# A recurrent scan's VectorE steps, joined over two heads and traced later

## Chip, cores and metric

The kernel runs on one core of a Trainium2 chip. The metric is device time in microseconds (us) of one execution. The engines are TensorE (PE in the profile: matmuls; its weight loads are PEld), VectorE (DVE), ScalarE (ACT), GpSimd (POOL) and SyncE (SP, which only issues DMAs). Each engine runs its own list of instructions in the order in which the list was written, and waits at an instruction until what it needs is there.

## The reference

One decoder layer on a sequence of 1024 tokens of width 1024, in float32. It normalises x, projects it into eight groups of 1024 channels, mixes over time in two ways, gates and adds the two results, projects back and adds to x. A squared-ReLU MLP of width 4096 and a last norm follow.

```python
xa, ga, q, f, v, g, m_a, m_b = split(h @ w_in)
xa = causal_depthwise_conv(xa)
# RG-LRU: a linear recurrence over time, channel by channel
r = sigmoid(blocks(xa, w_r) + b_r);  i = sigmoid(blocks(xa, w_i) + b_i)
log_a = -8 * r * softplus(-lam);     a = exp(log_a)
u = sqrt(max(-expm1(2 * log_a), 0)) * (i * xa)
h_t = a_t * h_(t-1) + u_t
y_a = h * gelu(ga)
# HGRN2: gated linear attention with 8 heads, decay f per key channel
o = rms_norm(hgrn2(silu(q), k(f), log f(f), v))
y_b = o * silu(g)
x = x + (sigmoid(m_a) * y_a + sigmoid(m_b) * y_b) @ w_out
```

## The kernel before

**Passes and pairs.** Time is cut into two passes `c` of 512 tokens (`NC`). In each pass a loop over `p` (L695) handles four pairs: 256 channels, that is two "heads" `s` of 128 channels (one per partition) by 512 tokens. After the four pairs comes the output projection of the pass (`out_proj`), and after both passes the MLP.

**Products.** Every float32 product is made from three matmuls of rounded parts, `mm3` (L123 to L125): high by high, high by low, low by high. The weights are loaded raw and cut into a high part by ACT (L78, names `wH`) and a low part by DVE (L79, names `wL`), three weight tiles ahead; a new raw tile is loaded when an old one has been cut.

**One pair, in PE's order.** PE's instructions within a pair are pinned to the order in which they are traced (`pin`, L117): the `q` projection, two steps of `f`, the RG-LRU's gate products `pr` and `pi` for both heads (L350 to L356), the rest of `f`; then the generator `gates` yields the projections `g`, `mb`, `ga`, `ma` in steps of six matmuls, and `hgrn` places its own small matmuls between them: `GO` says how many steps go ahead of each. The small ones are the first batch of scores (`blocks`, L415, three sets), the second batch (L533 and L544), the transposes `pk` (L570), the state products `pkv` (L579) and the outputs `po` (L603 and L606). L544 multiplies `kk` and `qf`, which DVE writes at L525 and L526 and ACT at L523 and L524. L606 reads the states `sn`, which DVE writes at L587 and L589.

**What orders the other engines.** The framework writes each engine's list at build, by a planner with estimated durations: whenever an engine is free it takes, of the instructions whose inputs are there, the one that was traced first. `high_priority(n)` counts an instruction as traced n earlier. The weight cuts have 400, and the RG-LRU has 300 (L707), ahead of everything else of its pair. The lists are fixed at run time.

**The RG-LRU** (`rg_lru`, L347 to L376). For each head: ACT computes the sigmoid of `pr` and its tanh into `w` (L358, L359) and the sigmoid of `pi` into `ig` (L361). DVE takes the maximum with 0 (L363), adds 1 (L365), takes the reciprocal (L366); ACT takes the square root of `w` (L367); DVE multiplies by the convolved input (L368), forms 2 w rec (L369), multiplies (L370), forms 2 rec - 1 (L371) and runs the scan along time (L373). POOL carries the last value into the next pass (L375). `w`, `ig` and `rec` are 128x512 tiles with one buffer each (tags `rw`, `ri`, `rr`), so head 1 follows head 0. Only L655 in `gates` reads the result `h`.

**The score chain** (`f_of`, L389, and `hgrn`, L402 to L558). DVE forms the decays `f` (L397, L399), then a long chain of products (all through the helper at L405) that scales queries and keys for the score levels; after the first batch of scores it copies those into `dd` (L426, L434), and writes `kk` and `qf` (L525, L526), `t64` and `t128` (L552, L558). POOL copies `dd` into the score matrix `scT` (L510), which L603 reads.

**Buffers.** A tile in a tag with one buffer has to wait until the last reader of the tile before it in that tag is done. The tags `rw` and `ri` also hold the states `sn` (L582), `rr` also holds a transposed key tile (L573), `on` holds the attention output (L561) and `g1` a gate (L635).

Of the kernel before, what the change touches and what calls it, by code (L numbers as in the profile page):

```python
# [13 lines left out]
AF = mybir.ActivationFunctionType  # L14
ALU = mybir.AluOpType
# [3 lines left out]
P = 128  # L19
D = 1024  # L20
S = 1024
T = 512
# [16 lines left out]
PV_LB, PV_CB, PV_BR, PV_BI, PV_LAM, PV_CW, PV_HG = 0, 8, 16, 24, 32, 40, 72  # L39
# [4 lines left out]
def trunk(ctx: ExitStack, tc: tile.TileContext, x, wts, mlp, pv, gains, mask_f, mask_u, out):  # L44
    nc = tc.nc
    V, A, G, PE = nc.vector, nc.scalar, nc.gpsimd, nc.tensor
# [13 lines left out]
    def bank(tag, name):  # L60
        return ps.tile([P, 512], F32, tag=tag, name=name, bufs={"pj": 4, "sc": 2, "hg": 2}[tag])
# [49 lines left out]
    def next_w():  # L111
        used[0] += 1
        return get_w(used[0] - 1)
# [3 lines left out]
    def pin(ins):  # L117
        if pinned[0]:
            tc.keep_in_program_order(ins)

    def mm3(o, ah, al, bh, bl, first, last, goes_on=False):
        how = {"skip_group_check": True} if goes_on else {}
        pin(PE.matmul(o, ah, bh, start=first, stop=False, **how))  # L123
        pin(PE.matmul(o, ah, bl, start=False, stop=False, **how))  # L124
        pin(PE.matmul(o, al, bh, start=False, stop=last, **how))  # L125
# [4 lines left out]
    pvt = const.tile([P, PV_N], F32, tag="pvt", name="pvt")  # L130
# [26 lines left out]
    def a2_set(pool, name):  # L157
        return [
            [pool.tile([P, 4, T], F32R, tag="a2", name=f"{name}{q}{h}", bufs=4) for h in range(2)] for q in ("H", "L")
        ]  # L160
# [17 lines left out]
    def mt(tag, name, shape=(P, T), dt=F32, bufs=1):  # L178
        return m.tile(list(shape), dt, tag=tag, name=name, bufs=bufs)
# [4 lines left out]
    def small_inputs():  # L184
        nc.sync.dma_start(pvt, pv)
        nc.sync.dma_start(mf, mask_f)
        mu32 = mt("kT", "mu32", (P, 4, P)).rearrange("p a b -> p (a b)")[:, : 7 * 32]
        mu32 = mu32.rearrange("p (i b t) -> p i b t", i=7, b=1)
        nc.sync.dma_start(mu32, mask_u)
        return mu32  # L190
# [5 lines left out]
    lb, omlb, sp4 = par[:, 0, :], par[:, 1, :], par[:, 2, :]  # L196
# [35 lines left out]
    hcar = const.tile([P, 8], F32, tag="hcar", name="hcar")  # L232
# [10 lines left out]
    def first_norm(c):  # L243
        dst = a2_set(a2h, f"hT{c}")
        xts = []
        for tt in range(4):
            r = c * 4 + tt
            xt = mt(X_TAGS[tt], f"x{r}", (P, D)) if c == 0 else tile_x(f"x{r}")
            nc.sync.dma_start(xt, x[r * P : (r + 1) * P, :])
            xts.append(xt)  # L250
            if c == 0 and tt == 0:
                gain0.append(gain_tile(0))
            if c == 0 and tt < 3:
                raws.append(load_w(seq[tt]))
        xns = {}

        def rows(tt):
            xns[tt] = mt("f" if tt % 2 == 0 else "tmp", f"xn{c}{tt}", (P, D))
            norm_rows(xts[tt], xns[tt], gain0[0], f"x{c}{tt}")

        def weights(n):
            if c == 0:
                fill_w(n)

        rows(0)
        weights(1)
        transposed(xns[0], dst, 0, f"x{c}0")
        rows(1)
        weights(2)
        for tt in range(1, 4):  # L270
            if tt < 3:
                rows(tt + 1)
            transposed(xns[tt], dst, tt, f"x{c}{tt}")
        weights(3)
        in_order[0] = False
        hT.append(dst)
# [14 lines left out]
    def run(steps, n=None):  # L291
        while n is None or n > 0:
            try:
                next(steps)
            except StopIteration as end:
                return end.value
            if n is not None:
                n -= 1

    def project(c, name):  # L300
        return run(project_steps(c, name))
# [44 lines left out]

    def rg_lru(c, p, xc, xh, xl):  # L347
        wh, wl = next_w()
        hs = mt("h", f"h{c}{p}", (P, 2, T))
        for s in range(2):  # L350
            u = 2 * p + s
            pr, pi = bank("pj", f"pr{c}{u}"), bank("pj", f"pi{c}{u}")
            for o, k0 in ((pr, 0), (pi, 2)):
                for k in range(2):
                    cols = slice((k0 + k) * 256 + s * P, (k0 + k) * 256 + (s + 1) * P)
                    mm3(o, wh[:, cols], wl[:, cols], xh[:, k, :], xl[:, k, :], k == 0, k == 1)  # L356
            w = mt("rw", f"rw{c}{u}")
            A.activation(w, pr, AF.Sigmoid, bias=pvt[:, PV_BR + u : PV_BR + u + 1])  # L358
            A.activation(w, w, AF.Tanh, scale=sp4[:, u : u + 1])  # L359
            ig = mt("ri", f"ri{c}{u}")  # L360
            A.activation(ig, pi, AF.Sigmoid, bias=pvt[:, PV_BI + u : PV_BI + u + 1])  # L361

            V.tensor_scalar(w, w, 0.0, None, op0=ALU.max)  # L363
            rec = mt("rr", f"rr{c}{u}")
            V.tensor_scalar(rec, w, 1.0, None, op0=ALU.add)  # L365
            V.reciprocal(rec, rec)  # L366
            A.activation(w, w, AF.Sqrt)  # L367
            V.tensor_tensor(out=ig, in0=ig, in1=xc[:, s, :], op=ALU.mult)  # L368
            V.scalar_tensor_tensor(w, w, 2.0, rec, op0=ALU.mult, op1=ALU.mult)  # L369
            V.tensor_tensor(out=ig, in0=ig, in1=w, op=ALU.mult)  # L370
            V.tensor_scalar(rec, rec, 2.0, -1.0, op0=ALU.mult, op1=ALU.add)  # L371
            h = hs[:, s, :]
            V.tensor_tensor_scan(h, rec, ig, hcar[:, u : u + 1], op0=ALU.mult, op1=ALU.add)  # L373
            if c + 1 < NC:
                G.tensor_copy(hcar[:, u : u + 1], h[:, T - 1 : T])  # L375
        return hs  # L376
# [22 lines left out]
        V.tensor_scalar(ff, ff, F_MIN, 1.0, op0=ALU.max, op1=ALU.min)  # L399
        return ff, kk  # L400

    def hgrn(c, p, q1, f, kk, v, go):  # L402

        nm = f"{c}{p}"
        mul = lambda o, a, b: V.tensor_tensor(out=o, in0=a, in1=b, op=ALU.mult)  # L405
# [67 lines left out]
        g0, g1 = 256 // c0, 256 // c1  # L473
# [35 lines left out]
        for b in range(4):  # L509
# [5 lines left out]
                op0=ALU.mult,  # L515
                op1=ALU.add,
# [41 lines left out]
        mul(t128, t64[:, 0::2], t64[:, 1::2])  # L558


        on = mt("on", f"on{nm}", (P, 8, P))  # L561
        ssq = mt("hssq", f"hssq{nm}", (P, 16), bufs=2)[:, 0:8]
        nkv = 3 if c + 1 == NC else 4
# [13 lines left out]
        for s, _ in both:  # L577
            for n in range(nkv):
                pin(PE.matmul(pkv[s][:, n * P : (n + 1) * P], kT[s][:, n, :], vn(s, n), start=True, stop=True))  # L579
        states = []  # L580
        for s, u in both:
            sn = mt(("rw", "ri")[s], f"sn{c}{u}", (P, 4, P))  # L582
            states.append([scar[:, u, :]] + [sn[:, n, :] for n in range(4)])
            for n in range(nkv):
                kv = pkv[s][:, n * P : (n + 1) * P]
                if c == 0 and n == 0:
                    V.tensor_copy(states[s][1], kv)  # L587
                else:
                    V.scalar_tensor_tensor(  # L589
                        states[s][n + 1],  # L590
                        states[s][n],
                        t128[:, 4 * s + n : 4 * s + n + 1],
                        kv,
                        op0=ALU.mult,
                        op1=ALU.add,
                    )
# [91 lines left out]
    for c in range(NC):  # L688
        if c == 0:
            first_norm(0)  # L690
            mu32 = small_inputs()
        else:
            out_proj(0, ys, res0, done0, lambda: first_norm(1))
        ys = a2_set(a2y, f"y{c}")
        for p in range(NPAIR):  # L695
            v = project_v(c, f"{c}{p}")
            px = project(c, f"xa{c}{p}")
            if c == 0 and p == 0:
                parameters()
                tc.keep_in_program_order(V.tensor_copy(mu, mu32.to_broadcast([P, 7, 8, 32])))  # L700
            xc3 = conv(c, p, px)
            pinned[0] = True
            q1 = q_of(c, p, project(c, f"q{c}{p}"))
            steps = project_steps(c, f"f{c}{p}")
            run(steps, 2)
            got = {}
            with tc.high_priority(300):  # L707
                got["h"] = rg_lru(c, p, *xc3)
            f, kk = f_of(c, p, run(steps))
            rest = gates(c, p, got, ys)  # L710
            got["on"] = hgrn(c, p, q1, f, kk, v, lambda n: run(rest, n))
            run(rest)
            pinned[0] = False
    mix.__exit__(None, None, None)
# [208 lines left out]
    for q in range(QUADS):  # L923
        n = q + 1 if q + 1 < QUADS else QUADS + QUADS - 2
# [79 lines left out]
    for kb in range(n_kb):  # L1004
        last = kb + 1 == n_kb
        qs = order[2 * kb : 2 * kb + 2]
        for half in range(2):
# [8 lines left out]
            for step, (bk, wo, uo), prs in [  # L1016
# [11 lines left out]
                for pr in prs:  # L1028
                    _, ci, cj, op = ADDS[step]
# [89 lines left out]
```

## Time and profile before

| | |
|---|---|
| median of 3 runs | 1598.83 us |
| lowest, highest | 1598.44, 1599.68 us |
| the profiled execution | 1599.54 us |
| its span | 1597.7 us |
| busy: PE, DVE, ACT, POOL | 1562.3, 1207.3, 771.7, 65.1 us |
| mean granted clock of PE | 0.995 |

The profile is one execution. Its rows give the start from the beginning of the span, the duration, the engine, the line of the kernel, the operation, the tiles written and read, and in square brackets the time that the engine idled before the instruction with what released it. Tile names are shown without their numbers, so one name stands for the tiles of all pairs. A group row gives a count and the shortest, median and longest duration in ns. The first pass runs from the start to about 490 us, the second to about 910, the MLP after that. A pair takes 104.8 us.

### The profile page before, as it was taken

Reading aid. Unit: us, or ns where it says so; the run is one execution under the profiler, and the core shown is the slowest. Engines: PE = TensorE matmul, PEld = TensorE weight load, DVE = VectorE, ACT = ScalarE, POOL = GpSimd, SP = SyncE. Lnnn points to the kernel's source line nnn. Section 1 sums busy time; section 2 is a strip of 40 time slices with the busy share of each in tenths; the row PEclk is TensorE's granted clock in tenths of the full one; section 3 lists DMA queues with packets and bytes.
Section 4 is the critical chain, followed back from the end, with each engine's and each line's share of the span. In section 5 each row is a group of like instructions: output and inputs, shape, how many; then the busy total and the mean of one; then the engine's idle time right before and its main releaser. Section 6 shows DMA issues by size and latency. Waiting matters only on the chain.

```text
span 1597.7 us, 23216 instructions
## 1 busy us (share of the span) xinstructions
PE 1562.3 (98%) x9240; PEld 1307.4 (82%) x9240; DVE 1207.3 (76%) x1751; ACT 771.7 (48%) x1210; POOL 65.1 (4%) x107
## 2 busy tenths in 40 slices
PE   7999999999999999999999998999999999999998
PEld 6888888888888888888888876888888878888886
DVE  5985966858764875947859787988888888888877
ACT  4643545446443544546435566767767732221113
POOL 0010010100100010100100100000000000000000
PEclk9999999999999999999999998999999999999999
DMA  6222213222254322322222462666666675666652
GB/s 239 95 67 94 95 64 105 81 87 87 84 166 133 97 76 82 104 76 97 67 95 92 141 206 89 266 256 242 237 250 257 224 270 229 256 248 256 257 203 106
DMA packets 57996, 246.51 MB, mean 154 GB/s; under 512 B 6688, under 2 KB 6816, under 8 KB 47136
## 3 DMA queue, kind: packets, MB, share of 16 engines
q1 hardware_dynamic: 56304, 239.27, 41.6%
q10 hardware_dynamic: 1584, 5.77, 1.0%
q8 instruction: 72, 1.18, 0.3%
q14 instruction: 36, 0.29, 0.1%
HBM read 185.24 MB, written 59.77 MB: 153 GB/s over the span
## 4 chain that ended last, share of the span: by engine, by line
PE 80%; DVE 14%; DMA 2%; ACT 2%; issue 2%; POOL 0%; DVEq 0%; POOLq 0%; SPq 0%; ACTq 0%
PE dX L123 3%; PE dX L124 3%; PE dX L125 3%; PE uX L123 3%; PE uX L124 3%; PE uX L125 3%; PE pj_ma L125 2%; PE pj_ma L123 2%; PE pj_xa L123 2%; PE pj_xa L124 2%; PE pj_ma L124 2%; PE pj_xa L125 2%; PE pv L125 2%; PE pv L124 2%; PE pj_f L125 2%; PE pj_q L125 2%
## 5 line engine op out<-in xcount | busy, mean ns | idle before, releaser
L79 DVE TENSOR_TENSOR wL<-raw,wH 128x1024 fp32r<-128x1024 f32 x160 | 194.9, 1218 | 134.6 <-ACT wH L78 133.0
L78 ACT CAST wH<-raw 128x1024 fp32r<-128x1024 f32 x160 | 167.6, 1048 | 124.3 <-PE po L124 31.7
L1031 DVE TENSOR_TENSOR acc<-acc,dX 128x512 f32<-128x512 f32 x128 | 85.0, 683 | 29.4 <-PE dX L125 28.8
L78 ACT CAST wA<-q 128x512 fp32r<-128x512 f32 x32 | 19.8, 621 | 135.0 <-PE dX L125 101.4
L1031 DVE TENSOR_TENSOR acc<-acc,dY 128x512 f32<-128x512 f32 x64 | 43.5, 685 | 15.7 <-PE dY L125 14.5
L366 DVE RECIPROCAL rr<-rr 128x512 f32<-128x512 f32 x16 | 53.5, 3345 | 0.0
L891 ACT ACTIVATE b<-b 128x512 f32<-128x512 f32 x48 | 30.2, 630 | 37.1 <-DVE b L890 37.1
L123 PE MATMUL pv<-wH,hT0H 128*128 128x256 f32 x128 | 37.2, 291 | 0.0
L124 PE MATMUL pv<-wL,hT0H 128*128 128x256 f32 x128 | 36.9, 288 | 0.0
L125 PE MATMUL pv<-wH,hT0L 128*128 128x256 f32 x128 | 36.8, 288 | 0.0
L123 PE MATMUL pv<-wH,hT1H 128*128 128x256 f32 x128 | 36.5, 285 | 0.0
L125 PE MATMUL pv<-wH,hT1L 128*128 128x256 f32 x128 | 36.2, 283 | 0.0
L124 PE MATMUL pv<-wL,hT1H 128*128 128x256 f32 x128 | 36.2, 283 | 0.0
L332 DVE SCALAR_TENSOR_TENSOR xc<-xp,pvt,xc 128x512 f32<-128x512 f32 x48 | 33.1, 745 | 0.0
L892 ACT ACTIVATE b<-b 128x512 f32<-128x512 f32 x48 | 30.0, 630 | 1.1
L79 DVE TENSOR_TENSOR wA<-q,wA 128x512 fp32r<-128x512 f32 x32 | 22.0, 688 | 10.7 <-ACT wA L78 10.1
L510 POOL TENSOR_SCALAR scT<-dd 32x256 f32<-32x256 f32 x32 | 25.4, 793 | 71.4 <-DVE dd L434 63.0
L123 PE MATMUL pj_ga<-hT0H,wH 128*128 128x512 f32 x64 | 27.1, 423 | 0.0
L523 ACT COPY kk<-kc 128x512 f32<-128x512 f32 x8 | 5.0, 623 | 45.3 <-DVE kc L405 45.3
L123 PE MATMUL pj_ga<-hT1H,wH 128*128 128x512 f32 x64 | 26.6, 416 | 0.0
L314 ACT COPY v<-pv 128x256 f32<-128x256 f32 x32 | 11.9, 370 | 29.5 <-PE pv L125 29.5
L632 ACT ACTIVATE smb<-pj_mb 128x512 f32<-128x512 f32 x16 | 9.6, 599 | 34.1 <-PE pj_mb L125 34.1
(1861 smaller groups left out, 5254.2 us busy)
## 6 DMA issues: line engine op xcount, KB each, us to landing
raw<-wts_in SPq DMA_DIRECT2D x160, 512.0 KB, 3.5
q<-mlp_in SPq DMA_DIRECT2D x64, 512.0 KB, 4.0
x<-x_in SPq DMA_DIRECT2D x8, 512.0 KB, 6.0
acc<-x ACTq DMA_DIRECT2D x8, 512.0 KB, 5.2
y_out<-acc SPq DMA_DIRECT2D x16, 256.0 KB, 2.0
xs<-x_in SPq DMA_DIRECT2D x8, 256.0 KB, 3.2
x<-xs SPq DMA_DIRECT2D x8, 256.0 KB, 2.5
x2s<-x_in SPq DMA_DIRECT2D x4, 512.0 KB, 5.2
```

The costliest lines, as they stand in the source:

```text
L78: keep(A.copy(h, src))
L79: keep(V.tensor_tensor(out=lo, in0=src, in1=h.bitcast(F32), op=ALU.subtract))
L123: pin(PE.matmul(o, ah, bh, start=first, stop=False, **how))
L124: pin(PE.matmul(o, ah, bl, start=False, stop=False, **how))
L125: pin(PE.matmul(o, al, bh, start=False, stop=last, **how))
L314: A.copy(v[:, tt, :], pp[:, :256])
L332: V.scalar_tensor_tensor(xc[:, s, :], xp[:, j : j + T], pvt[:, PV_CW + 8 * j + u : PV_CW + 8 * j + u + 1], xc[:, s, :], op0=ALU.mult, op1= ...
L366: V.reciprocal(rec, rec)
L510: G.tensor_scalar(scT[32 * b : 32 * b + 32, :, 32 * b : 32 * b + 32], dd[32 * b : 32 * b + 32, :, :], 1.0, 0.0, op0=ALU.mult, op1=ALU.add,)
L891: A.activation(b[:, at, :], b[:, at, :], AF.Relu, scale=-1.0 if at == 2 else 1.0)
L892: A.activation(b[:, at, :], b[:, at, :], AF.Square)
L1031: V.tensor_tensor(out=dst, in0=dst, in1=banks[bk, pr], op=op)
```

## The change

`rg_lru` keeps PE's products and ACT's three gate activations, now into tiles that hold both heads (`w` in tag `rw`, `ig` in tag `on`), and returns them. A new function `rg_scan` has DVE's part and one square root over both heads; the reciprocal and the scan stay one per head. `rec` lies in the tag `g1`, `h` is allocated there too. `hgrn` calls `rg_scan` after `t128` (L558), outside the high priority. The states of both heads share one tile in tag `rw`; the tag `ri` is gone.

```diff
     def rg_lru(c, p, xc, xh, xl):
         wh, wl = next_w()
-        hs = mt("h", f"h{c}{p}", (P, 2, T))
+        w = mt("rw", f"rw{c}{p}", (P, 2, T))
+        ig = mt("on", f"ri{c}{p}", (P, 2, T))
         for s in range(2):
...
-            w = mt("rw", f"rw{c}{u}")
-            A.activation(w, pr, AF.Sigmoid, bias=pvt[:, PV_BR + u : PV_BR + u + 1])
-            A.activation(w, w, AF.Tanh, scale=sp4[:, u : u + 1])
-            ig = mt("ri", f"ri{c}{u}")
-            A.activation(ig, pi, AF.Sigmoid, bias=pvt[:, PV_BI + u : PV_BI + u + 1])
-
-            V.tensor_scalar(w, w, 0.0, None, op0=ALU.max)
-            rec = mt("rr", f"rr{c}{u}")
-            V.tensor_scalar(rec, w, 1.0, None, op0=ALU.add)
-            V.reciprocal(rec, rec)
-            A.activation(w, w, AF.Sqrt)
-            V.tensor_tensor(out=ig, in0=ig, in1=xc[:, s, :], op=ALU.mult)
-            V.scalar_tensor_tensor(w, w, 2.0, rec, op0=ALU.mult, op1=ALU.mult)
-            V.tensor_tensor(out=ig, in0=ig, in1=w, op=ALU.mult)
-            V.tensor_scalar(rec, rec, 2.0, -1.0, op0=ALU.mult, op1=ALU.add)
+            A.activation(w[:, s, :], pr, AF.Sigmoid, bias=pvt[:, PV_BR + u : PV_BR + u + 1])
+            A.activation(ig[:, s, :], pi, AF.Sigmoid, bias=pvt[:, PV_BI + u : PV_BI + u + 1])
+            A.activation(w[:, s, :], w[:, s, :], AF.Tanh, scale=sp4[:, u : u + 1])
+        return w, ig, xc
+
+    def rg_scan(c, p, w, ig, xc):
+        V.tensor_scalar(w, w, 0.0, None, op0=ALU.max)
+        rec = mt("g1", f"rr{c}{p}", (P, 2, T))
+        V.tensor_scalar(rec, w, 1.0, None, op0=ALU.add)
+        A.activation(w, w, AF.Sqrt)
+        for s in range(2):
+            V.reciprocal(rec[:, s, :], rec[:, s, :])
+        V.tensor_tensor(out=ig, in0=ig, in1=xc, op=ALU.mult)
+        V.scalar_tensor_tensor(w, w, 2.0, rec, op0=ALU.mult, op1=ALU.mult)
+        V.tensor_tensor(out=ig, in0=ig, in1=w, op=ALU.mult)
+        V.tensor_scalar(rec, rec, 2.0, -1.0, op0=ALU.mult, op1=ALU.add)
+        hs = mt("h", f"h{c}{p}", (P, 2, T))
+        for s in range(2):
+            u = 2 * p + s
             h = hs[:, s, :]
-            V.tensor_tensor_scan(h, rec, ig, hcar[:, u : u + 1], op0=ALU.mult, op1=ALU.add)
+            V.tensor_tensor_scan(h, rec[:, s, :], ig[:, s, :], hcar[:, u : u + 1], op0=ALU.mult, op1=ALU.add)
...
-    def hgrn(c, p, q1, f, kk, v, go):
+    def hgrn(c, p, q1, f, kk, v, go, scan):
...
         mul(t128, t64[:, 0::2], t64[:, 1::2])
+        scan()
...
+        sn2 = mt("rw", f"sn{c}{p}", (P, 2, 4, P))
         for s, u in both:
-            sn = mt(("rw", "ri")[s], f"sn{c}{u}", (P, 4, P))
+            sn = sn2[:, s]
...
             with tc.high_priority(300):
-                got["h"] = rg_lru(c, p, *xc3)
+                rg = rg_lru(c, p, *xc3)
             f, kk = f_of(c, p, run(steps))
             rest = gates(c, p, got, ys)
-            got["on"] = hgrn(c, p, q1, f, kk, v, lambda n: run(rest, n))
+            def scan():
+                got["h"] = rg_scan(c, p, *rg)
+            got["on"] = hgrn(c, p, q1, f, kk, v, lambda n: run(rest, n), scan)
```

## Prediction

> **What bounds the kernel now.** I read the page's busy shares first.
>
> ```profile
> PE 1562.3 (98%) x9240; PEld 1307.4 (82%) x9240; DVE 1207.3 (76%) x1751; ACT 771.7 (48%) x1210; POOL 65.1 (4%) x107
> ```
>
> PE has work 98% of the span; VectorE (DVE) is idle a quarter of it. A DVE edit is worth only the time that PE waits for DVE. So next the stages that the change touches, one window for a pair of pass 0, one for the last pair of pass 0, one for a pair of pass 1 (columns: length, then busy time and instructions of PE, PEld, DVE, ACT, POOL, then PE's granted clock):
>
> ```profile
> 70.00:175.00 105.00, 104.53 (x758) 89.44 (x757) 75.09 (x114) 51.10 (x86) 7.74 (x13) 1.00 0.26 86
> 385.00:440.00 55.00, 53.12 (x478) 44.73 (x477) 44.07 (x77) 26.40 (x53) 6.39 (x11) 0.97 0.27 86
> 650.00:755.00 105.00, 105.00 (x757) 89.42 (x756) 74.91 (x113) 50.88 (x86) 5.87 (x7) 1.00 0.27 86
> ```
>
> The reader sees how little there is: PE idles 0.47 us in a pair of pass 0, 1.88 us in its last pair, nothing in pass 1. The list of PE's waits in pass 0 says for what:
>
> ```profile
> PE sc L544 <- DVE dd L434: 1.5, 3, 0.5
> PE sc L544 <- ACT wH L78: 1.0, 1, 1.0
> PE sc L533 <- DVE qb L405: 0.9, 1, 0.9
> ```
>
> All are at the second batch of scores. Then the timeline there, PE and DVE of the second pair (start, duration, idle before):
>
> ```profile
> 203.63 0.70 PE L533 MATMUL sc<-qb,kc 128*32 128x32 f32 x32
> 204.82 1.12 PE L544 MATMUL sc<-qf,kk 128*64 128x64 f32 x16 [0.49 <-DVE dd L434]
> ```
>
> ```profile
> 162.04 0.43 DVE L363 TENSOR_SCALAR rw<-rw 128x512 f32<-128x512 f32 x1 [2.90 <-ACT rw L359]
> ...
> 172.61 0.69 DVE L368 TENSOR_TENSOR ri<-ri,xc 128x512 f32<-128x512 f32 x1 [0.76 <-ACT ri L361]
> 173.60 1.22 DVE L79 TENSOR_TENSOR wL<-raw,wH 128x1024 fp32r<-128x1024 f32 x1 [0.29 <-ACT wH L78]
> ...
> 176.26 3.34 DVE L366 RECIPROCAL rr<-rr 128x512 f32<-128x512 f32 x1
> ...
> 184.19 0.67 DVE L399 TENSOR_SCALAR f<-f 128x1024 f32<-128x1024 f32 x1
> ...
> 200.12 0.21 DVE L405 TENSOR_TENSOR seg<-seg 128x16 f32<-128x16 f32 x1
> ...
> 203.99 0.68 DVE L405 TENSOR_TENSOR qf<-qb,seg 128x512 f32<-128x512 f32 x1
> ...
> 206.67 0.88 DVE L405 TENSOR_TENSOR qf<-qf,seg 128x512 f32<-128x512 f32 x1
> ```
>
> L544 multiplies qf (L526); qf ends at 203.99 + 0.68 = 204.67 and L544 starts 0.15 later. (The wait is put down to dd, but L544 does not read dd.) PE could have gone on at 203.63 + 0.70 = 204.33. From 162.04 to 204.67 DVE is one unbroken queue but for 0.76 + 0.29 us: RG-LRU first, then the score chain from L399. **The end of that queue sets PE's stall**, 0.49 us. In pass 1 the same place is just in time:
>
> ```profile
> 673.68 0.68 DVE L405 TENSOR_TENSOR qf<-qb,seg 128x512 f32<-128x512 f32 x1
> 673.91 0.70 PE L533 MATMUL sc<-qb,kc 128*32 128x32 f32 x32
> 674.54 0.33 PE L544 MATMUL sc<-qf,kk 128*64 128x64 f32 x2
> ```
>
> qf ends at 674.36; with the 0.15 us of above that is 0.03 us of slack. Nothing can be gained in pass 1, and any delay shows.
>
> **The change part by part.** *Fewer, longer DVE instructions.* The rows of the RG-LRU operations (median in ns), and two that are 1024 wide:
>
> ```profile
> L365 DVE TENSOR_SCALAR rr<-rw x16: 416/424/428, 57.6 to 854.5; 128x512 f32<-128x512 f32 x16
> L366 DVE RECIPROCAL rr<-rr x16: 3343/3344/3347, 58.6 to 855.2; 128x512 f32<-128x512 f32 x16
> L369 DVE SCALAR_TENSOR_TENSOR rw<-rw,rr x16: 676/677/679, 62.9 to 859.5; 128x512 f32<-128x512 f32 x16
> L370 DVE TENSOR_TENSOR ri<-ri,rw x16: 680/683/686, 64.6 to 860.6; 128x512 f32<-128x512 f32 x16
> L373 DVE TENSOR_TENSOR_SCAN h<-rr,hcar,ri x16: 1275/1280/1286, 65.7 to 861.9; 128x512 f32<-128x512 f32 x16
> L405 DVE TENSOR_TENSOR on<-on,hrs x8: 1225/1225/1227, 117.7 to 900.8; 128x1024 f32<-128x1024 f32 x8
> L655 DVE SCALAR_TENSOR_TENSOR g<-g,h x8: 1224/1224/1225, 114.7 to 897.7; 128x1024 f32<-128x1024 f32 x8
> ```
>
> Removed per head: three scalar forms (L363, L365, L371) at 0.42, the reciprocal 3.34, two products 0.68, L369 0.68, the scan 1.28 = 7.92; two heads 15.84 us in 16 instructions. Added per pair: three scalar forms 1024 wide at 0.67 (L399's row is that form), two reciprocals 6.68, two products at 1.225, one of L655's form at 1.22, two scans 2.56 = 14.92 us in 10. That saves 0.92 us. Independent neighbours overlap by some 0.08 us (173.60 + 1.22 = 174.82, and the next starts at 174.74), and six instructions fewer lose six overlaps: 0.44 at the other end. I take 0.7.
>
> *A later start.* The first DVE step now needs both heads. ACT and PE rows:
>
> ```profile
> 161.28 0.73 ACT L359 ACTIVATE rw<-rw,par 128x512 f32<-128x512 f32 x1
> ...
> 162.63 1.28 ACT L367 ACT_TABLE_LOAD   x1
> ...
> 170.24 0.69 ACT L358 ACTIVATE rw<-pr,pvt 128x512 f32<-128x512 f32 x1 [0.81 <-DVE ri L370]
> ```
>
> ```profile
> 162.79 0.39 PE L125 MATMUL pr<-xcH,wL 128*128 128x512 f32 x1
> ```
>
> Head 1's L358 can start when its last product ends, 162.79 + 0.39 = 163.18 (before, it waited 0.81 us for head 0's tile); with 0.69 for L358 and 0.73 for L359 the tanh of head 1 ends at 164.6, with the hand-overs 164.7. Head 0's ended at 162.01 and DVE began at 162.04. The whole block therefore starts 2.66 us later. Against that the two idle gaps go, since head 1 has its own tiles: 1.05 us.
>
> *The order on DVE.* The order is made at build: at each moment the ready instruction that was traced earliest, moved up by any priority. Tracing the block later does not push it behind the score chain; it only loses the moments in which something traced earlier is ready. Where a chain step isn't ready, a later one goes in: L552 (t64) runs at 200.12, ahead of L525 and L526 that were traced before it. The block is ready at 164.7, some ten microseconds before f. So the reciprocals still run ahead of the chain; the rest goes into its gaps and into the moment in which the chain waits for the first scores. All of it then lies ahead of qf again, and qf's end moves by +2.66 - 1.05 - 0.7 = +0.91; by the bounds of the saving 0.69 to 1.17. If the last scan alone slips behind qf (1.28 - 0.08) it is -0.3. Between those I stay near the first, since both scans are ready before the first scores are, and take 0.75.
>
> *Sum.* Pass 0, first three pairs: 3 x 0.75 = 2.2. Pass 1, four pairs: 4 x (0.75 - 0.03) = 2.9. The last pair of pass 0 has its own trouble, the next pass's norm inside its score chain:
>
> ```profile
> 410.39 1.28 DVE L147 SCALAR_TENSOR_TENSOR xn<-x,rstd_x,gain 128x1024 f32<-128x1024 f32 x1 [0.38 <-POOL rstd_x L146]
> ...
> 415.90 1.55 PE L544 MATMUL sc<-qf,kk 128*64 128x64 f32 x16 [0.97 <-ACT wH L78]
> ```
>
> It may move out (a gain: 0.49 as elsewhere, 1.5 for L147's time and wait less an overlap, and 1.5 of half clock, below: 3.5) or stay (a loss of 0.75). I take 0. Sum +5.1 us.
>
> *Costed at nothing.* One square root instead of two removes two of four 1.28 us table loads a pair: ACT is 48% busy and releases nothing that PE waits for here. The new slots: the states of L582 wait until w is done, ig sits in "on" (next written after the scores are applied, 214.60 below), rec in "g1" (next written at L639). If the block is done by qf's end, all have over 6 us. hcar's copies share POOL with the score copies:
>
> ```profile
> L510 POOL TENSOR_SCALAR scT<-dd 32x256 f32<-32x256 f32 x32 | 25.4, 793 | 71.4 <-DVE dd L434 63.0
> ```
>
> Four of these, 3.2 us from about 204.8 (after the last score copy), against some 214.2 when scT is read, just ahead of L606's 214.60 below: 6 us of cover. No DMA moves. The weight splits (L79) keep their priority, so SP's loads are freed as before, at worst one reciprocal (3.3 us) later, as now.
>
> [...] After the last pair's waits the clock halves:
>
> ```profile
> 417.00:418.00 1.00, 1.00 (x7) 0.50 0.00 0
> ```
>
> ```profile
> 207.36 1.03 PE L570 MATMUL pk<-ident,kk 128*128 128x128 f32 x8
> ```
>
> ```profile
> 419.97 1.03 PE L570 MATMUL pk<-ident,kk 128*128 128x128 f32 x8
> ```
>
> From L544 to L570 it takes 4.07 us there and 2.54 in the second pair: 1.5 us for waits of 0.92 and 0.97. [...]
>
> **Rivals.**
> 1. *The last steps slip behind qf* (the other side: faster). If both scans are placed after L526, qf ends 0.75 - 2 x 1.20 = -1.65 us, that is 1.65 earlier: the three stalls of 0.49 go (-1.5), the last pair gains 1.6 to 3.5, pass 1 nothing. -3.1 to -5.0; on the scale of the median 1594 to 1596. It wins from 0.75 us slipped per pair. For it: low priority; against it: t64's row, a gap is filled by whatever is ready.
> 2. *Nothing moves where it counts*: later start and savings cancel, within 2 us of now, 1599.
> 3. *Stalls long enough for half clock*: +1.5 us in each of seven pairs on top of 5.1: +15.6, 1614. Against it: 0.49 us stalls leave the clock at 1.00.
> 4. *The block really runs behind the chain.* Then it starts at 206.67 + 0.88 = 207.55; w is free after 11.1 us (0.67 x 2, 6.68, 1.22 x 3, less overlaps), and states must follow:
>
> ```profile
> 211.88 1.36 DVE L589 SCALAR_TENSOR_TENSOR sn<-sn,seg,pkv 128x128 f32<-128x128 f32 x4
> ```
>
> ```profile
> 214.60 0.28 PE L606 MATMUL po<-sn,qf 128*128 128x128 f32 x1
> ```
>
> The row is head 1's three states, the head before it takes about as long: 2.7 us from 218.65 is 221.4, where L606 stood at 214.60. That is 7 us a pair, 10 if the scans (3.2 us with L371's form) go ahead of the states too: +55 to +80, half clock beside it, 1655 to 1690.
>
> **How the numbers follow.** The profiled execution took 1599.54 us, span 1597.70, 0.71 above the median 1598.83 of the three runs; on the median's scale 1598.83 + 5.1 = 1603.9. Chances: forecast (+1.5 to +9) 0.50, rival 1 0.28, rival 2 0.09, rival 3 0.07, rival 4 0.06. The bound of a measurable difference is 0.2%, 3.2 us. Faster by more: 0.20 (most of rival 1). Within: 0.24 (the rest of rival 1, rival 2, the low end of the forecast). Slower: 0.56. Range: from rival 1's far end, 1594, to 1612, where the forecast's upper bound 8 x 1.17 meets half clock in a pair or two; rivals 3 and 4 are mostly left out.
>
> **What would show it.** DVE's max starts near 164.7 in the second pair, not 162.0. Reciprocals before L399. Position of the scans against L526: before it, qf ends near 205.4 and PE waits about 1.2 us at L544 in pass 0 and 0.7 in pass 1; after it, no wait. Wrong if L147 leaves the last pair's chain (3 us back), if the clock falls in other pairs, or if L606 waits for states.

## The result, and the profile after

| | before | after |
|---|---|---|
| median, lowest, highest of 6 runs, us | 1598.63, 1596.32, 1600.22 | 1606.84, 1604.79, 1608.64 |
| the profiled execution, its span, us | 1599.54, 1597.7 | 1608.64, 1606.8 |

The ratio is 1.0051, with a 95% interval of 1.0038 to 1.0064: the change costs 8.2 us. The two profiled executions are 9.1 us apart, a little more than the medians. In the changed kernel the lines behind the RG-LRU stand lower: the second scores are L538 and L549 (were L533 and L544), the helper of the chain is L410 (was L405), the transposes L576, the clamp of f L404.

The page of the changed kernel, busy time by engine:

```profile
PE 1562.4 (97%) x9240; PEld 1306.6 (81%) x9240; DVE 1200.3 (75%) x1703; ACT 748.8 (47%) x1186; POOL 92.7 (6%) x107
```

DVE did lose 7.0 us of work, 0.9 a pair, and ACT 22.9, 2.9 a pair. PE's work is the same; the span is longer because PE waits more. POOL's busy time rose by 27.6 us, which the prediction's sum doesn't have (experiment 6 says where). The same three windows as before (length, then busy time of PE, PEld, DVE, ACT, POOL, then PE's granted clock, the DMA's share and its GB/s):

```profile
70.00:175.00 105.00, 103.34 (x753) 88.37 (x752) 73.20 (x108) 46.98 (x81) 12.69 (x13) 1.00 0.24 84
385.00:440.00 55.00, 52.42 (x479) 44.22 (x478) 47.56 (x79) 25.14 (x52) 12.12 (x12) 1.00 0.25 87
650.00:755.00 105.00, 104.03 (x754) 88.69 (x753) 72.98 (x106) 47.41 (x82) 9.92 (x7) 1.00 0.24 85
```

PE now idles 1.66 us where it idled 0.47, and 0.97 in the pair of pass 1 that had no idle time. Its list of waits names the second scores again (total, times, longest; the other waits of either list are at the norms and in the MLP):

```profile
PE sc L549 <- DVE dd L439: 6.3, 7, 1.0
PE sc L538 <- DVE qb L410: 3.6, 4, 1.6
PE sc L549 <- ACT wH L78: 1.0, 1, 1.0
```

That is 10.9 us against 3.4 before, so 7.5 of the 9.1 us stand in three rows. The prediction put the whole stall at the product of `qf` (L544, now L549); the product of `qb` ahead of it (L538) waits as well. The timeline of the second pair, PE first and then DVE:

```profile
205.66 0.86 PE L538 MATMUL sc<-qb,kc 128*32 128x32 f32 x32 [0.53 <-DVE qb L410]
207.32 1.12 PE L549 MATMUL sc<-qf,kk 128*64 128x64 f32 x16 [0.81 <-DVE dd L439]
```

```profile
166.11 0.69 DVE L364 TENSOR_SCALAR rw<-rw 128x1024 f32<-128x1024 f32 x1 [5.55 <-ACT rw L360]
...
172.92 3.34 DVE L369 RECIPROCAL rr<-rr 128x512 f32<-128x512 f32 x1
...
178.93 0.68 DVE L404 TENSOR_SCALAR f<-f 128x1024 f32<-128x1024 f32 x1
...
197.43 1.28 DVE L378 TENSOR_TENSOR_SCAN h<-rr,hcar,ri 128x512 f32<-128x512 f32 x1
...
201.29 1.28 DVE L378 TENSOR_TENSOR_SCAN h<-rr,hcar,ri 128x512 f32<-128x512 f32 x1
...
206.49 0.69 DVE L410 TENSOR_TENSOR qf<-qb,seg 128x512 f32<-128x512 f32 x1
...
209.17 0.88 DVE L410 TENSOR_TENSOR qf<-qf,seg 128x512 f32<-128x512 f32 x1
```

The reader sees one queue without a gap from 166.11 on, with both scans ahead of qf, the second of them inside the chain that follows the first scores. qf ends at 207.18 and L549 starts 0.14 later, as before the change. The pair as a whole lies 1.41 us later than before (first scores at 197.16, then 195.75), so against its own pair DVE starts at 164.70 and qf ends 1.10 us later. In pass 1, the sixth pair:

```profile
679.60 0.70 PE L538 MATMUL sc<-qb,kc 128*32 128x32 f32 x32
...
681.26 1.12 PE L549 MATMUL sc<-qf,kk 128*64 128x64 f32 x16 [0.97 <-DVE dd L439]
```

Here L538 still finds its operands and L549 waits. One pair has more than a wait: in the third pair PE's clock is halved (0.50), which before the change happened in the fourth:

```profile
316.00:317.00 1.00, 1.00 (x4) 0.73 (x3) 0.23 (x1) 0.00 (x0) 0.90 (x2) 0.50 0.93 360
317.00:318.00 1.00, 1.00 (x7) 0.80 (x6) 0.00 (x0) 0.00 (x0) 0.00 (x0) 0.72 0.22 82
...
417.00:418.00 1.00, 1.00 (x7) 0.81 (x6) 1.00 (x3) 0.00 (x0) 0.00 (x0) 1.00 0.00 0
```

**Where the 9.1 us went.** The distance from one pair's first scores to the next's, read from the timeline of either kernel, adds the waits up:

| from pair to pair | 1-2 | 2-3 | 3-4 | 4-5 (over the pass) | 5-6 | 6-7 | 7-8 |
|---|---|---|---|---|---|---|---|
| before, us | 104.83 | 104.81 | 104.79 | 152.84 | 104.57 | 104.61 | 104.58 |
| after, us | 106.09 | 105.90 | 107.60 | 152.49 | 105.47 | 105.44 | 105.30 |
| difference | +1.26 | +1.09 | +2.81 | -0.35 | +0.90 | +0.83 | +0.72 |

That is 7.3 us up to the last pair; 0.15 stands ahead of the first, and 1.7 behind the last pair's first scores, of which 0.7 is that pair's own wait (L549 there 12.49 us after the first scores, 11.76 before). The last 1.0 us lies behind the pairs, where PE's transposes for the MLP's norm wait for DVE (before, then after; total, times, longest):

```profile
PE xT_h L772 <- DVE xn_h L147: 1.1, 2, 0.8
```

```profile
PE xT_h L784 <- DVE xn_h L147: 2.3, 3, 1.7
```

One of these waits is 1.73 us where it was 0.84. In the profiles of the experiments below it is anything from 0.69 us (in a slower run, 5) to 1.88 (in a faster one, 2), so it does not follow the waits in the pairs.

### The profile page after: what moved, and what is told of

Read it like the earlier page. It is cut to its first block, busy times and chain, and to the rows that moved or that the text cites. A ratio compares the mean times of both kernels' runs of the same rounds, so it can differ in the third digit from the quotient of the medians.

```text
span 1606.8 us, 23139 instructions
## 1 busy us (share of the span) xinstructions
PE 1562.4 (97%) x9240; PEld 1306.6 (81%) x9240; DVE 1200.3 (75%) x1703; ACT 748.8 (47%) x1186; POOL 92.7 (6%) x107
## 4 chain that ended last, share of the span: by engine, by line
PE 78%; DVE 15%; issue 2%; ACT 2%; DMA 1%; POOL 1%; DVEq 0%; POOLq 0%; ACTq 0%; SPq 0%
PE dX L123 3%; PE dX L124 3%; PE dX L125 3%; PE uX L123 3%; PE uX L125 3%; PE uX L124 3%; DVE wL L79 2%; PE pj_ma L125 2%; PE pj_ma L123 2%; PE pj_xa L123 2%; PE pj_xa L124 2%; PE pj_ma L124 2%; PE pv L123 2%; PE pv L124 2%; PE pj_f L123 2%
## 5 line engine op out<-in xcount | busy, mean ns | idle before, releaser
L79 DVE TENSOR_TENSOR wL<-raw,wH 128x1024 fp32r<-128x1024 f32 x160 | 195.4, 1221 | 132.3 <-ACT wH L78 130.6
L468 POOL TENSOR_SCALAR seg<-seg 128x128 f32<-128x128 f32 (+1 forms) x16 | 31.6, 1974 | 443.9 <-DVE seg L410 443.9
L364 DVE TENSOR_SCALAR rw<-rw 128x1024 f32<-128x1024 f32 x8 | 5.5, 694 | 43.7 <-ACT rw L360 43.7
L79 DVE TENSOR_TENSOR wA<-q,wA 128x512 fp32r<-128x512 f32 x32 | 22.0, 687 | 10.1 <-ACT wA L78 9.8
```

Source lines behind the costliest of these rows:

```text
L79: keep(V.tensor_tensor(out=lo, in0=src, in1=h.bitcast(F32), op=ALU.subtract))
L468: G.tensor_scalar(after[:, :, 2], t4[:, :, 3], 1.0, 0.0, op0=ALU.mult, op1=ALU.add)
```

## The experiments

**Theory A**: DVE's queue ends later, because the joint block can only start when both heads are ready and all of it still lies ahead of qf; PE waits for qf. **Theory B**: the joint, 1024 wide operations cost something by themselves, by slowing GpSimd beside them. **Theory C**: the low place in the trace is the cost. All runs were timed against the kernel before.

**1. The join alone, in the old place.**

```diff
             with tc.high_priority(300):
                 rg = rg_lru(c, p, *xc3)
+                got["h"] = rg_scan(c, p, *rg)
...
-            got["on"] = hgrn(c, p, q1, f, kk, v, lambda n: run(rest, n), scan)
+            got["on"] = hgrn(c, p, q1, f, kk, v, lambda n: run(rest, n), lambda: None)
```

> The joint block, put back into its old place ahead of f with its old priority of 300. Theory A (VectorE's queue end sets the stall: a later start of 2.66 us, and both scans ahead of qf): the start stays late (max near 166 in pair 2), but with the high priority at least one scan of 1.2 us finds its place elsewhere than in the score chain, so qf ends about where it did before the change: 1598 to 1602. Theory B (the joint, wide operations cost by themselves, on VectorE or by slowing GpSimd beside them): it stays near the changed kernel, 1604 to 1608. Theory C (the low place in the trace is the cost): 1596 to 1600.

1607.07 us, ratio 1.0051 (1.0038 to 1.0063): the same as the changed kernel. Theory C falls. The time is where theory B put it and not where A did; runs 3 and 4 tell the two apart. What failed of A is the hope for the scans: with the priority they ran at 183.24, ahead of f, and the wait moved forward to the first scores:

```profile
200.45 0.89 PE L420 MATMUL sc<-qb,kc 128*32 128x48 f32 x64 [1.72 <-DVE qb L410]
```

The place within the queue ahead of qf decides only where PE waits.

**2. The move alone.** The block stays behind `t128`, but head by head.

```diff
-    def rg_scan(c, p, w, ig, xc):
-        V.tensor_scalar(w, w, 0.0, None, op0=ALU.max)
...
+    def rg_scan(c, p, w2, ig2, xc):
+        rec2 = mt("g1", f"rr{c}{p}", (P, 2, T))
         hs = mt("h", f"h{c}{p}", (P, 2, T))
         for s in range(2):
...
+            w, ig, rec, h = (t[:, s, :] for t in (w2, ig2, rec2, hs))
+            V.tensor_scalar(w, w, 0.0, None, op0=ALU.max)
...
+            A.activation(w, w, AF.Sqrt)
...
```

> The block traced behind the score chain as in the change, but head by head with 512 wide operations and two square roots, each head with its own half of the tiles. Theory A (late start and queue length): head 0 starts near 162 again and the two idle gaps of 1.05 us are gone, so qf ends about 1 us earlier than before the change: the three stalls of 0.49 us of pass 0 go, 1595 to 1599. Theory C (the low place in the trace is the cost): 1603 to 1607, as the changed kernel. Theory B (width): 1597 to 1600.

1596.82 us, ratio 0.9989 (0.9980 to 0.9998). DVE starts at 161.51 in the second pair and L549 (L548 here) doesn't wait:

```profile
203.81 1.12 PE L548 MATMUL sc<-qf,kk 128*64 128x64 f32 x16
```

So the later place, with a half tile of its own for each head, is a small gain; what costs is in the join.

**3. The late start alone.** As in 2, with head 0's steps queued behind head 1's maximum. No operation is joint.

```diff
+        first = V.tensor_scalar(w2[:, 1, :], w2[:, 1, :], 0.0, None, op0=ALU.max)
         for s in range(2):
...
+            if s == 0:
+                with tc.issue_after(first.ins):
+                    V.tensor_scalar(w, w, 0.0, None, op0=ALU.max)
+                    V.tensor_tensor(out=ig, in0=ig, in1=xc[:, s, :], op=ALU.mult)
```

> The block head by head behind the score chain, which took 1596.8, with one thing changed: all of head 0's VectorE steps are queued behind head 1's maximum, so that VectorE starts when both heads are ready, as in the change, but with no joint operation and two square roots. Theory A (the late start and what it pushes into the score chain): 1602 to 1608, with waits of PE at both score batches. Rival (the joint, wide operations or their shared square root cost something by themselves): 1595 to 1600.

1605.28 us, ratio 1.0036 (1.0024 to 1.0049): 8.5 us slower by the medians, 7.5 by the ratios, than run 2, which differs only in where these steps are queued.

```profile
165.51 0.43 DVE L366 TENSOR_SCALAR rw<-rw 128x512 f32<-128x512 f32 x1 [5.55 <-ACT rw L360]
```

```profile
204.75 0.90 PE L542 MATMUL sc<-qb,kc 128*32 128x32 f32 x32 [0.27 <-DVE qb L414]
206.42 1.12 PE L553 MATMUL sc<-qf,kk 128*64 128x64 f32 x16 [0.77 <-DVE dd L443]
```

The same two waits stand there, with no wide operation and two square roots.

**4. The early start given back, the rest joint.**

```diff
-        V.tensor_scalar(w, w, 0.0, None, op0=ALU.max)
...
+        for s in range(2):
+            V.tensor_scalar(w[:, s, :], w[:, s, :], 0.0, None, op0=ALU.max)
+            V.tensor_scalar(rec[:, s, :], w[:, s, :], 1.0, None, op0=ALU.add)
+            V.reciprocal(rec[:, s, :], rec[:, s, :])
         A.activation(w, w, AF.Sqrt)
```

> The changed kernel with maximum, sum and reciprocal head by head, so that VectorE starts on head 0 near 162 in pair 2 and not near 165; the square root, both products, the decay and the place in the trace stay joint as in the change. Theory A (the start that waits for both heads): qf ends 2 us or more earlier than in the changed kernel: 1594 to 1599. Theory B (the wide operations themselves, by slowing GpSimd's segment copies): 1603 to 1608. One square root saves or costs nothing in either.

1598.85 us, ratio 1.0001 (0.9992 to 1.0010): the loss is gone, with the three wide products of L370 to L372 and the single square root still there. DVE starts at 162.36. Runs 3 and 4 together settle A against B.

**5. Width, and the square root.** In one run L370 to L372 go head by head, in another only the square root does.

```diff
+        for s in range(2):
+            V.tensor_tensor(out=ig[:, s, :], in0=ig[:, s, :], in1=xc[:, s, :], op=ALU.mult)
...
```

```diff
-        A.activation(w, w, AF.Sqrt)
+        for s in range(2):
+            A.activation(w[:, s, :], w[:, s, :], AF.Sqrt)
```

> The changed kernel with the three 1024 wide operations behind the reciprocals (L370 to L372) made head by head, 512 wide; the joint start, the one square root and the place in the trace stay. Theory A (the joint start): 1605 to 1609, as the changed kernel or one more from three extra instructions a pair. Theory B (width): 1598 to 1603.

> The changed kernel with a square root for each head again, so two table loads more a pair on ScalarE. Theory A (ScalarE has room; the square root is not on the path): 1605 to 1609, as the changed kernel. If the single square root saves time that PE sees, it is 2 or more slower: over 1609.

Width: 1604.03 us, ratio 1.0034 (1.0021 to 1.0047), between the two expectations. The interval overlaps that of the changed kernel, so a cost of the width is not shown. The waits are nearly those of the changed kernel:

```profile
205.08 0.94 PE L539 MATMUL sc<-qb,kc 128*32 128x32 f32 x32 [0.42 <-DVE qb L411]
206.75 1.12 PE L550 MATMUL sc<-qf,kk 128*64 128x64 f32 x16 [0.72 <-DVE dd L440]
```

The first three pairs and the step over the pass are 3.8 us shorter in this profile, of which 1.4 is the third pair's half clock, absent here (from the second pair's first scores to the fourth's it takes 211.53 us, and in the changed kernel 213.50, which is 212.1 without the 1.4); pass 1 is not shorter. One product of head 0 also runs at 163.57, in time in which DVE otherwise idles for the joint start. The square root: 1606.24 us, ratio 1.0045 (1.0033 to 1.0058), no difference from the changed kernel that the intervals could tell.

**6. GpSimd's segment copies on ScalarE.**

```diff
-            G.tensor_scalar(after[:, :, 2], t4[:, :, 3], 1.0, 0.0, op0=ALU.mult, op1=ALU.add)
+            A.copy(after[:, :, 2], t4[:, :, 3])
```

> The changed kernel with the segment copies of L468 on ScalarE in place of GpSimd, where they took 0.96 us at the median beside the wide VectorE operations. Theory A: only kc's waits on them go, 0.3 us in two pairs: 1605.5 to 1607. Theory B (the contention of the wide operations with GpSimd is what delays the chain): 1599 to 1604.

1604.53 us, ratio 1.0034 (1.0022 to 1.0046), again between the two: 2.3 us below the changed kernel, though the intervals overlap. qf ends 0.20 to 0.43 us earlier in each pair (9.78 us after the first scores in the second pair, 10.02 in the changed kernel). The third pair's half clock is absent here too (211.31 us from the second pair's first scores to the fourth's), 1.4 us of the difference between the two profiles.

The 0.96 us of the expectation is a median over copies of two sizes. The 128x128 copy took 4.9 us in five pairs of the changed kernel and 1.7 us in three, 0.43 in all eight before; that is 26 of the 27.6 us that POOL was busier. What runs beside it can be read from the rows. Before the change it was a gate product that reads PSUM (POOL, then DVE):

```profile
189.31 0.43 POOL L463 TENSOR_SCALAR seg<-seg 128x128 f32<-128x128 f32 x1 [4.41 <-DVE seg L405]
```

```profile
189.12 0.70 DVE L628 TENSOR_TENSOR g<-g,pj_g 128x512 f32<-128x512 f32 x1
```

After the change L371 has come into that place. In the second pair the copy ends beside a weight cut (L79), which takes 1.45 us and not 1.22:

```profile
185.13 1.66 POOL L468 TENSOR_SCALAR seg<-seg 128x128 f32<-128x128 f32 x1 [35.31 <-DVE seg L410]
```

```profile
184.94 1.23 DVE L371 SCALAR_TENSOR_TENSOR rw<-rw,rr 128x1024 f32<-128x1024 f32 x1
...
186.41 1.45 DVE L79 TENSOR_TENSOR wL<-raw,wH 128x1024 fp32r<-128x1024 f32 x1
```

In the fourth pair it lasts until DVE stands idle for it:

```profile
398.61 4.93 POOL L468 TENSOR_SCALAR seg<-seg 128x128 f32<-128x128 f32 x1 [35.29 <-DVE seg L410]
```

```profile
403.57 0.96 DVE L410 TENSOR_TENSOR kc<-kb,seg 128x768 f32<-128x768 f32 x1 [0.32 <-POOL seg L468]
```

DVE's `kc` needs the copy and waits for it in five pairs, 1.6 us in all; in the other three the weight cut takes 0.23 us longer. But it isn't width: with the 512 wide products of run 5 the copy takes 4.41 us in the second pair, and in run 9, the fastest, 4.41. Nor does the copy make the loss: run 3 has it at 0.43 us in the second pair and loses, run 4 at 4.39 and does not.

**7. Both scans behind qf.** This is the prediction's first rival, made to happen.

```diff
-        mul(pairs(qf)[:, :, 1, :], q8[:, :, 1, :], t8[:, :, 0:1].to_broadcast([P, 16, 32]))
+        last_q = mul(pairs(qf)[:, :, 1, :], q8[:, :, 1, :], t8[:, :, 0:1].to_broadcast([P, 16, 32]))
...
+            with tc.issue_after(last_q.ins):
+                V.tensor_tensor_scan(h, rec[:, s, :], ig[:, s, :], hcar[:, u : u + 1], op0=ALU.mult, op1=ALU.add)
```

> The changed kernel with both scans (L378, 1.2 us each) queued behind qf's last step on VectorE. Theory A: qf ends 2 x 1.2 us earlier than in the changed kernel, that is 1.3 us earlier than before the change; PE waits at neither score batch, about 8 x 1.0 to 1.7 us are gained against the changed kernel: 1594 to 1597, faster than both. If the wait moves to the states (L596) or to the next block behind the late scans, or if GpSimd's slow segment copies set kc's end (theory B), it stays at 1600 to 1607.

1608.80 us, ratio 1.0061 (1.0048 to 1.0074). The expectation failed, though qf did end 8.72 us after the first scores and not 10.02. The scans now stand ahead of the halving of `kk`, which the transposes need; timeline of DVE and PE, second pair:

```profile
206.03 2.68 DVE L379 TENSOR_TENSOR_SCAN h<-rr,hcar,ri 128x512 f32<-128x512 f32 x2
...
209.91 0.68 DVE L411 TENSOR_TENSOR kk<-kk,seg 128x512 f32<-128x512 f32 x1
```

```profile
210.64 1.09 PE L577 MATMUL pk<-ident,kk 128*128 128x128 f32 x8 [1.68 <-DVE kk L411]
```

**8. Both scans behind the last halving of qf**, two DVE steps further.

```diff
-        mul(halves(qf)[:, :, 1, :], halves(qf)[:, :, 1, :], t16[:, :, 0:1].to_broadcast([P, 8, 64]))
+        last_q = mul(halves(qf)[:, :, 1, :], halves(qf)[:, :, 1, :], t16[:, :, 0:1].to_broadcast([P, 8, 64]))
```

> The changed kernel with both scans (2 x 1.2 us) queued on VectorE behind the last halving of qf (the step after t64), where PE's transposes of kk no longer need VectorE. With them behind qf's first step the wait at the second scores went, but PE waited 10.1 us in 8 pairs for kk's halving at the transposes instead. Theory A (queue position is what costs): neither wait, 1594 to 1598, 9 to 13 below the changed kernel. Rival: the wait moves once more, to the states and to L611, which need the VectorE steps behind the scans: 1601 to 1608.

1595.53 us, ratio 0.9977 (0.9968 to 0.9986): with the joint block and its late start, and still faster than both kernels. The scans fill a gap in which DVE waits for PE's state products:

```profile
207.16 2.45 DVE L379 TENSOR_TENSOR_SCAN h<-rr,hcar,ri 128x512 f32<-128x512 f32 x2
210.26 0.29 DVE L595 COPY sn<-pkv 128x128 f32<-128x128 f32 x1 [0.66 <-PE pkv L586]
```

After 2.45 us of scans DVE still idles 0.66 us before the states; nothing waits for them.

**9. The same with the other blocks.** The scans of run 2 and of run 4 behind the last halving.

```diff
-            V.tensor_tensor_scan(h, rec, ig, hcar[:, u : u + 1], op0=ALU.mult, op1=ALU.add)
+            with tc.issue_after(last_q.ins):
+                V.tensor_tensor_scan(h, rec, ig, hcar[:, u : u + 1], op0=ALU.mult, op1=ALU.add)
```

> The block head by head behind the score chain (1596.8 as measured), and both scans behind the last halving of qf. Theory A: the remaining waits of PE at the scores (0.8 and 0.8 us) go and the queue gains 2.4 us that nothing waits for: 1593 to 1597, at best 2 us under the kernel before. Rival (wait moves to the states): 1598 to 1605.

> Maximum, sum and reciprocal head by head (early start), the rest joint with one square root, and both scans behind qf's last halving. Theory A: PE waits for VectorE at neither score batch, and nothing is left to gain there: 1593 to 1596, the same as with the late start and the scans behind (1595.5), since a wait that is gone can't go twice. If the start still mattered with the scans out of the way, it would be 2 or more below 1595.5.

Head by head: 1594.59 us, ratio 0.9969 (0.9957 to 0.9981), the fastest run of this study. Early start with the joint products: 1595.11, ratio 0.9979 (0.9969 to 0.9990). In neither does PE wait at the second scores; the second pair of the first of the two:

```profile
203.19 0.70 PE L538 MATMUL sc<-qb,kc 128*32 128x32 f32 x32
203.81 1.15 PE L549 MATMUL sc<-qf,kk 128*64 128x64 f32 x16
```

The intervals of runs 8 and 9 overlap: once the wait is gone (run 8 keeps 0.3 us of it in two pairs, 0.85 in the fourth), the start and the join make no difference that could be told. A good part of the gain on the kernel before is in its troubled fourth pair: the next pass's norm, which ran at 410.39 inside the score chain, runs at 402.98 ahead of the first scores, and the step over the pass takes 149.40 us instead of 152.84.

**10. PE later instead of DVE earlier.** The changed kernel with one number changed.

```diff
-GO = (17, 4, 1, 1, 2)
+GO = (17, 5, 1, 1, 2)
```

> The changed kernel with one number changed in PE's order: five projection steps and not four between the first scores and the second (GO[1] 4 to 5), so one step of six products at 0.23 us, 1.37 us, is taken from behind and put ahead of L538. VectorE's queue is untouched. Theory A (VectorE's qb and qf end 0.5 to 1.6 us too late for PE): PE finds other work in that time, and most of the 9.9 us of waits at L538 and L549 go: 1595 to 1601. Rival (the time is lost elsewhere, or the taken step opens a wait behind, at the end of the pair): 1603 to 1608.

1595.73 us, ratio 0.9984 (0.9975 to 0.9993). DVE's queue is untouched, qf even ends 10.19 us after the first scores, but PE has 1.37 us of projection to do meanwhile:

```profile
204.84 0.70 PE L538 MATMUL sc<-qb,kc 128*32 128x32 f32 x32
205.93 1.12 PE L549 MATMUL sc<-qf,kk 128*64 128x64 f32 x16 [0.39 <-DVE dd L439]
```

**One rule behind all runs.** From each profile's timeline: when qf's first step ends and when the product that reads it starts, both counted in us from the pair's first scores (second pair), and qf's end in the sixth pair.

| run | qf ends, pair 2 | its product starts | qf ends, pair 6 | ratio to before |
|---|---|---|---|---|
| kernel before | 8.92 | 9.07 | 11.60 | 1 |
| kernel after | 10.02 | 10.16 | 12.50 | 1.0051 |
| 1 join in the old place | 9.60 | 10.42 | 12.24 | 1.0051 |
| 2 move alone | 8.44 | 8.59 | 10.50 | 0.9989 |
| 3 late start alone | 9.71 | 9.86 | 12.57 | 1.0036 |
| 4 early start, rest joint | 9.12 | 9.27 | 11.15 | 1.0001 |
| 5 products by head | 9.88 | 10.03 | 12.47 | 1.0034 |
| 5 two square roots | 10.17 | 10.32 | 12.54 | 1.0045 |
| 6 copies on ScalarE | 9.78 | 9.93 | 12.14 | 1.0034 |
| 7 scans behind qf | 8.72 | 8.87 | 10.33 | 1.0061 |
| 8 scans behind its halving | 8.72 | 8.87 | 10.49 | 0.9977 |
| 9 by head, scans there | 7.73 | 8.48 | 10.15 | 0.9969 |
| 9 early start, scans there | 7.77 | 8.52 | 10.18 | 0.9979 |
| 10 one more step on PE | 10.19 | 10.34 | 12.55 | 0.9984 |

The product starts 0.14 or 0.15 us after qf's end, or when PE itself arrives: 8.5 us in pass 0 (run 9, no wait), 11.6 in most pairs of pass 1. The exceptions are told above: run 1 waited earlier (1.72 us), run 7 later, run 10 moved PE's arrival by 1.37 us.

## Why the prediction was right, and where its sizes were off

The forecast was +5.1 us, and +8.2 came. The mechanism is the one that was forecast; two sizes were not, and one term came out right by luck.

- **The later start**: 164.7 was forecast for DVE's first step in the second pair, 164.70 measured on that pair's clock. Run 3 shows that this alone makes a loss of this size (7.5 us against run 2), run 4 that without it there is none. Right.
- **Saving and gaps**: 0.7 us a pair was taken, and DVE's busy time fell by 0.9; both idle gaps are gone. Right.
- **The order**: reciprocals ahead of the chain, all of the block ahead of qf, as forecast. Tracing the block later did nothing by itself (run 1).
- **qf's end, taken as +0.75**: this is the term that was mis-sized. Against the first scores it moved by 1.24, 1.10 and 1.25 us in the first three pairs, and by 0.92, 0.90, 0.74 and 0.74 in pass 1. What the sum lacked is GpSimd's copy: the shifted order brought another DVE step beside it, and the copy costs DVE 0.2 to 0.3 us in every pair (experiment 6). With the copies on ScalarE qf's end moves by 0.82 to 0.86 us in the first three pairs, between the 0.75 that was taken and the 0.91 from which it was shaded, and by 0.5 in pass 1. Why it moves less in pass 1 is not shown.
- **First three pairs**: 2.2 us was the term, 5.2 came. The stalls are 3.7 of it (1.26, 1.09, and 1.4 of the 2.81), the half clock in the third pair the other 1.4: L549 to the transposes took 3.97 us there and 2.55 in the second pair. Rival 3 had this price, 1.5 us, but for seven pairs. A clock that falls in another pair was one of the prediction's signs of being wrong, and it came, once.
- **The fourth pair, taken as 0**: -0.35 came with the step over the pass, and that the terms cancel is luck. The norm stayed in the chain (416.38, between the first scores and qf), which the prediction had priced at +0.75: the wait at L538 grew from 0.92 to 1.61 us, and L549 starts 0.66 later. But the half clock of that pair went, -1.5, and 0.5 came in small steps at the output projection behind it. The half clock that left this pair and the one that came in the third nearly cancel. The norm's row after the change:

```profile
416.38 1.26 DVE L147 SCALAR_TENSOR_TENSOR xn<-x,rstd_x,gain 128x1024 f32<-128x1024 f32 x1
```

- **Pass 1**: 2.9 us for four pairs; 0.90, 0.83, 0.72 and 0.7 came, 3.2 in all. Right, though the slack of 0.03 us was not there: before the change the product starts at 11.75 to 11.78 us, held by qf, and PE alone comes at 11.6. So some 0.2 us a pair could be gained where the prediction saw nothing, and runs 2 and 8 gain it in most pairs (104.4 us from pair to pair, 104.6 before).
- **Costed at nothing**: the square root (run 5) and the new slots; PE waits nowhere for states or for scT. Right. That GpSimd lies on the path through `kc` was not seen.
- **Rival 1** had the right sign and price, 1594 to 1596 (run 8: 1595.5), but the wrong place. Behind L526, where the prediction put the scans, they stand ahead of the halving that the transposes need, and 1608.8 came of it (run 7). The step that failed is that only qf was looked at as what DVE's queue must deliver.

What stays open is why the clock halves in one pair and not in another, why qf's end moves less in pass 1, and what sets the wait at the MLP's norm.

## What to carry to other kernels

Joining two instructions saves some of their time (two products of 0.68 us became one of 1.22) but starts at the later of the two operands; where the queue behind has no slack, price the lost head start first (2.7 us here) and the saving second (0.9). In a list that is filled with whatever is ready, tracing work later doesn't put it later: to move it off a path, order it behind a named instruction, and choose that one by asking what PE needs next and next after that. And a wait of one engine can be closed from the other side as well: one projection step moved ahead of the waiting product was worth nearly as much as the best order on VectorE (ratio 0.9984 against 0.9969, with intervals that overlap).

## What the hardware showed

**GpSimd beside VectorE.** A copy of one column per head, two of them, took 6.85 us in run 1, and ended 0.15 us after VectorE had begun the gate product L635:

```profile
184.58 6.85 POOL L380 COPY hcar<-h 128x1 f32<-128x1 f32 x2 [34.76 <-DVE h L378]
```

```profile
191.28 0.70 DVE L635 TENSOR_TENSOR g<-g,pj_g 128x512 f32<-128x512 f32 x1
```

Before the change one such copy took 0.19 to 0.57 us. In run 9 the segment copy stood for 4.41 us, and let VectorE itself run dry before it ended (the wait of 0.31 us is for the copy):

```profile
183.20 4.41 POOL L468 TENSOR_SCALAR seg<-seg 128x128 f32<-128x128 f32 x1 [35.22 <-DVE seg L410]
```

```profile
187.64 0.96 DVE L410 TENSOR_TENSOR kc<-kb,seg 128x768 f32<-128x768 f32 x1 [0.31 <-POOL seg L468]
```

This copy ended 0.28 us after VectorE had run dry. In three pairs of the changed kernel the copy took 1.7 us and ended 0.38 us after a weight cut (L79) had begun, and that cut took 1.45 us and not 1.22 (experiment 6); in the other five it outlasted that cut and took 4.9 us. What holds the copies up, and why three pairs differ from five, is not shown.

**The clock.** In the changed kernel PE's clock halved in the third pair (0.50 from 315 to 317 us) after waits of 0.74 and 0.97 us, not in the first after 0.69 and 0.97, and not in the fourth after 1.61 and 0.97 (1.00 behind both); so the length of the waits does not decide it alone. Nor do the other runs settle it. With two square roots (run 5) the fourth pair has the same two waits, 1.61 and 0.97, and from L550 to the transposes it takes 3.98 us there and 2.54 in the second pair, so there the clock did fall. In run 1, behind waits of 1.72 and 1.71 us in the second and the fourth pair, and in run 7, behind 1.68 in the second, the products start 0.23 us apart as elsewhere. In run 10 no pair from the second on halves (2.54 to 2.58 us from L549 to the transposes), with waits of 0.85 us at most. Behind the pairs, where PE waits 5.54 us at a norm of the MLP, the clock does fall: 0.50 from 963 to 969 us before the change.
